# Moving the operand sums and two gate blocks of a Strassen stage into the attention heads before it

## The chip, the cores and the metric

One core of one Trainium2 chip. Times are device microseconds of that core. The kernel was timed in several runs, and one execution of it was taken by the hardware profiler; that one has a span, from its first instruction to its last, and a time of its own.

## The reference, cut to what matters

A block of an encoder on 1024 tokens of 1024 features, in float32. From a normed and modulated `h` one matrix product makes ten groups of 1024 columns, eight blocks of 128 each:

```
proj = h @ w_in[l]
(a_bg, a_cg, a_x, a_z, q, k, v, z_b, a_raw, b_raw, gate_a_raw, gate_b_raw) = split(proj)
ya = a_cg * dwconv_centred(a_bg * a_x, conv_a_w[l]);  ya = (ya * silu(a_z)) @ w_pa[l]
...   # q, k, v: convolution, silu, then 8 heads of a gated delta rule, in both directions: o
yb = (norm(o) * silu(z)) @ w_pb[l]
merged = sigmoid(gate_a_raw) * ya + sigmoid(gate_b_raw) * yb
x = x + gate * (merged @ w_o[l]);  return rmsnorm(x, final_norm_w)
```

## The kernel before, in words

Every large product is made in float32 accuracy from rounded parts: an operand is split into a high and a low part, and a product is three matmuls (high x high, high x low, low x high). The activations `h` lie in SBUF as `hhi`, `hlo` (8 tiles each). A plain block of 128 output columns takes 2 halves x 8 k x 3 = 48 matmuls of 128x512.

**The heads.** q, k, v and z of the eight heads, and the eight blocks of gate a (ga), are projected in plain blocks while the heads' recurrences run. Generators describe the work: `prep_k`, `prep_q`, `merge`, `chain`, `head_out` for each head (chain is the recurrence: 8 steps that go to and fro between TensorE, VectorE and ScalarE; merge completes a triangular inverse that GpSimd forms as many small operations on a tile E), and `fill()` (L1088), one stream of plain blocks. The class `Scheduler` (L59) runs them in Python against a model of costs and writes out a fixed order for each engine. TensorE takes the first stream that is ready, and `fill` stands behind all those of the heads; other engines take, of what is ready, the lowest priority number first. A stream can ask for ("need", name) and goes on when another stream has marked that name.

`fill` keeps a list of main jobs (k, q, v of the next heads, z of the last), each with needs, and a list of gates. `choose()` (L1105) picks the next job while the current one stands ahead; the weights of the job chosen are then loaded by `loader`:

```
share = (total - START - RESERVE) * (mains - len(jobs)) / mains + START
if gates and jobs and total - len(gates) < int(share):
    return gates.pop(0)
if jobs and (len(gates) <= RESERVE or all(n in sched.done for n in jobs[0][3])):
    return jobs.pop(0)
return gates.pop(0) if gates else None
```

The job chosen waits for its needs before its first matmul. z of head h-1 needs ("out", h-2), the mark of `head_out(h-2)` (L1098); z7, the last main job, needs ("out", 6). Its buffer has the tag "tmp" with two buffers, which v and z use in turn.

**The Strassen stage.** The groups bg, ax, cg, az (32 blocks) and two blocks of gate b are projected in pairs of blocks. `Pair` (L1201) makes a pair as seven products of 12 matmuls, 84 in place of 96. Weights are loaded raw (four DMAs a pair), summed (S1 to S4) on VectorE, and each operand is split: `prep` copies the high part on ScalarE, `rest` subtracts for the low part on VectorE, five products ahead (AHEAD). The activations need sums too, T1 to T4, in four rounds m: `sums(m)` (L1169) adds high and low parts of two k-tiles, subtracts four times, and splits the four results. These sums are formed behind the heads, one round beside each of the four plain blocks gb0 to gb3 (`gate_block`, L1367; weights by `wtile`); the loop is at L1374. Then 17 pairs follow, the last of gb4 and gb5, then plain gb6 and gb7, and the output stages.

The heads and this stage are two sections, each with an order of its own on VectorE, ScalarE, GpSimd and SP; rows of the two can interleave. SBUF of the heads (pools `gq`, `gp`) is given to the pools `bw`, `hxp`, `bt` of the stage behind them, tile by tile as readers end.

Of the kernel before, what the change touches and what calls it, by code (L numbers as in the profile page):

```python
# [8 lines left out]
F32 = mybir.dt.float32  # L9
# [315 lines left out]
def block(ctx: ExitStack, tc: tile.TileContext, x, c, wada, wadag, badaT, nwT, win, wab, cva, cvq,  # L325
# [118 lines left out]
    maskF = gc_.tile([P, P], F32, name="maskF")  # L444
    maskB = gc_.tile([P, P], F32, name="maskB")
# [11 lines left out]
    beta = gc_.tile([P, 16, NC], F32, name="beta")  # L457
    exps = gc_.tile([P, 3, 16, NC], F32, name="exps")
    negeg = gc_.tile([P, 16, NC], F32, name="negeg")
    neggc = gc_.tile([P, 16, NC], F32, name="neggc")  # L460
    eg, esuf, gl = exps[:, 0], exps[:, 1], exps[:, 2]

    gq = gctx.enter_context(tc.tile_pool(name="gq", bufs=1))
# [272 lines left out]

    gp = gctx.enter_context(tc.tile_pool(name="gp", bufs=1, reuse_waits="tile"))
# [7 lines left out]
    def big(tag, name, bufs=1):  # L745
        return tile_of(gp, [P, T], tag, name, bufs)
# [341 lines left out]
    def fill():  # L1088
        jobs = []
        for h in range(1, H + 1):  # L1090
            todo = {}
            if 1 < h < H:
                todo["q"] = (Q0 + h, f"q{h}", conv(h, "q", 0), [("chain_e", h - 2)])
            if h + 1 < H:
                todo["k"] = (K0 + h + 1, f"k{h + 1}", conv(h + 1, "k", 8), [("chain_e", h - 2)] if h > 1 else [])
            if h < H:
                todo["v"] = (V0 + h, f"v{h}", conv(h, "v", 16), [("pq", h - 1)])
            todo["z"] = (Z0 + h - 1, f"z{h - 1}", silu_z(h - 1), [("out", h - 2)] if h > 1 else [])  # L1098
            jobs += [todo[c] for c in JOBS if c in todo]
# [69 lines left out]
    def sums(m):  # L1169
        t = []  # L1170
        for k in (2 * m, 2 * m + 1):
            t.append(hxp.tile([P, T], F32, tag="hx", name=f"hx{k}"))
            (V if k % 2 else G).tensor_tensor(t[-1], hhi[k].bitcast(F32), hlo[k].bitcast(F32), ALU.add)
        b11, b12, b21, b22 = (x[:, ch(half, 512)] for x in t for half in range(2))
        V.tensor_tensor(b11, b12, b11, ALU.subtract)
        V.tensor_tensor(b12, b22, b12, ALU.subtract)
        V.tensor_tensor(b22, b22, b11, ALU.subtract)
        V.tensor_tensor(b21, b21, b22, ALU.subtract)
        for n, x in zip(SUMS, (b11, b22, b12, b21)):
            hi, lo = hop[n][m]  # L1180
            S.activation(hi, x, AF.Copy)
            (G if n == "T3" else V).tensor_tensor(lo, x, hi.bitcast(F32), ALU.subtract)
# [18 lines left out]
    class Pair:  # L1201
# [4 lines left out]
        def __init__(self, name, j0, consume, place=None):  # L1206
            self.name, self.consume, self.place = f"{name}{j0}", consume, place
            self.srcs = [win[DST[name] + j0 + b] for b in range(2)]
            self.raw, self.ops, self.banks, self.u = {}, {}, {}, {}
            self.order = {"first": ("A11", "S4", "S2", "A12", "S1", "S3", "A22"),  # L1210
                          "last": ("S2", "S1", "S3", "A22", "A11", "A12", "S4")}.get(place, tuple(RHS))

        def operand(self, n):
            if n not in self.raw:
                if n in ADDS:
                    x, y, op = ADDS[n]
                    x, y = self.operand(x), self.operand(y)
                    t = bw.tile([P, 512], F32, tag="sum", name=f"{n}_{self.name}", bufs=4)
                    V.tensor_tensor(t, x, y, op)
                    self.raw[n] = t  # L1220
                else:
                    for b, a in ((1, 0), (1, 1), (0, 0), (0, 1)):
                        t = bw.tile([P, 512], F32, tag="raw", name=f"wr_{self.name}{b}{a}", bufs=8)
                        Q.dma_start(t, self.srcs[b][:, ch(a, 512)])
                        self.raw[b, a] = t
            return self.raw[n]

# [10 lines left out]
        def product(self, n):  # L1238
            own = (self.place, n) in (("first", "S4"), ("last", "A12"), ("last", "S4"))
# [5 lines left out]
            hi, lo, _ = self.ops.pop(n)  # L1245
# [14 lines left out]
        def after(self, n, ps):  # L1260
# [26 lines left out]
            elif n == "A12":  # L1287
                self.consume(0, 0, ps, None)
# [75 lines left out]
    pairs += [stored("gb", j, sgb_d, AF.Sigmoid, "last" if j + 2 == LAST else None) for j in range(PLAIN[1], LAST, 2)]  # L1364
# [9 lines left out]
    plain = range(*PLAIN)  # L1374
    ws = [wtile(win[G_B + plain[0]], f"gb{plain[0]}")]
    for i, j in enumerate(plain):
        sums(i)
        if j + 1 in plain:
            ws.append(wtile(win[G_B + j + 1], f"gb{j + 1}"))
        else:  # L1380
            for s, (p, n) in enumerate(steps[:4]):
                p.prep(n)
                if s:
                    steps[s - 1][0].rest(steps[s - 1][1])
# [228 lines left out]
```

## Time and profile before

| | us |
|---|---|
| median of 3 runs | 1423.4 (1422.5 to 1424.5) |
| the profiled execution's own time | 1424.3 |
| its span | 1422.5 |
| TensorE busy (PE) | 1371.3, 96% |
| VectorE (DVE) | 852.1, 60% |
| ScalarE (ACT) | 606.6, 43% |
| GpSimd (POOL) | 499.6, 35% |

Time outside the span is 1.8 us in that execution. PE rows are matmuls, PEld their weight loads; a float32 matmul of 128 columns in the heads stands as two rows. Matmuls overlap, so their durations add up to more than the time from one start to the next. The granted clock has two levels, 1.00 (2.4 GHz) and 0.5 (1.2 GHz); a stretch shows a mean. L319 is the line of the helper that records all operations of the heads on engines other than TensorE, L213 that of their matmuls: there one goes by the tiles' names. A name before "<-" is written, those behind it are read; "wl" and "wh" are low and high parts of weights, "wr" raw weights.

### The profile page before, as it was taken

Reading aid. Unit: us, or ns where it says so; the run is one execution under the profiler, and the core shown is the slowest. Engines: PE = TensorE matmul, PEld = TensorE weight load, DVE = VectorE, ACT = ScalarE, POOL = GpSimd, SP = SyncE. Lnnn points to the kernel's source line nnn. Section 1 sums busy time; section 2 is a strip of 40 time slices with the busy share of each in tenths; the row PEclk is TensorE's granted clock in tenths of the full one; section 3 lists DMA queues with packets and bytes.
Section 4 is the critical chain, followed back from the end, with each engine's and each line's share of the span. In section 5 each row is a group of like instructions: output and inputs, shape, how many; then the busy total and the mean of one; then the engine's idle time right before and its main releaser. Section 6 shows DMA issues by size and latency. Waiting matters only on the chain.

```text
span 1422.5 us, 22420 instructions
## 1 busy us (share of the span) xinstructions
PE 1371.3 (96%) x8510; PEld 1145.9 (81%) x8510; DVE 852.1 (60%) x1496; ACT 606.6 (43%) x1490; POOL 499.6 (35%) x728
## 2 busy tenths in 40 slices
PE   6899999999999999998699999999999999999998
PEld 5678888887888887988587788788888788888886
DVE  6868174757686766766326676776767544422335
ACT  5447575565646473745343323232322431222211
POOL 2014837575738384747116100000000123455301
PEclk9999999999999999999899999999999999999999
DMA  9224341514150515132112312103030566665402
GB/s 354 97 70 144 117 95 56 149 39 141 33 146 31 127 54 135 45 75 60 46 45 90 133 45 84 65 24 110 15 119 30 213 231 237 222 200 170 178 16 104
DMA packets 123726, 154.41 MB, mean 109 GB/s; under 512 B 74593, under 2 KB 74977, under 8 KB 123618
## 3 DMA queue, kind: packets, MB, share of 16 engines
q1 hardware_dynamic: 123330, 152.19, 33.6%
q8 instruction: 67, 1.10, 0.3%
q10 hardware_dynamic: 288, 0.79, 0.1%
q14 instruction: 41, 0.34, 0.1%
HBM read 123.45 MB, written 29.50 MB: 108 GB/s over the span
## 4 chain that ended last, share of the span: by engine, by line
PE 46%; POOL 4%; DVE 2%; DMA 2%; issue 1%; ACT 1%; SPq 0%; POOLq 0%; ACTq 0%; DVEq 0%
PE ps_cg_S L1249 4%; PE ps_ax_S L1249 4%; PE ps_az_S L1249 3%; PE ps_bg_S L1249 3%; PE pp_pb L1150 2%; PE pp_pb L1152 2%; PE pp_pa L1152 2%; PE pp_pa L1150 2%; PE pp_pa L1151 2%; PE pp_pb L1151 2%; PE fo L1518 2%; PE fo L1517 2%; PE fo L1519 2%; PE ps_ax_A L1249 2%; PE ps_cg_A L1249 2%; PE pp_ga L213 1%
## 5 line engine op out<-in xcount | busy, mean ns | idle before, releaser
L1142 POOL TENSOR_TENSOR wl_gb<-wr_gb,wh_gb 128x512 fp32r<-128x512 f32 x12 | 19.5, 1646 | 347.8 <-ACT wh_gb L1141 347.8
L319 POOL TENSOR_TENSOR et<-E 128x30 f32<-128x30 f32 (+7 forms) x240 | 112.9, 471 | 28.7 <-DMA E<-s 12.2
L319 POOL TENSOR_TENSOR E<-E,et 128x30 f32<-128x30 f32 (+7 forms) x240 | 114.6, 478 | 17.2
L319 DVE SCALAR_TENSOR_TENSOR S<-S,exps,cb 128x128 f32<-128x128 f32 x96 | 29.7, 343 | 62.0 <-PE cb L213 61.3
L319 ACT ACTIVATE vw<-cb,cols 128x128 f32<-128x128 f32 x112 | 36.0, 364 | 59.1 <-PE cb L213 59.0
L213 PE MATMUL pp_z<-hlo,wh_z 128*128 128x512 f32 x128 | 52.7, 412 | 0.0
L213 PE MATMUL pp_z<-hhi,wl_z 128*128 128x512 f32 x128 | 52.6, 411 | 0.0
L213 PE MATMUL pp_z<-hhi,wh_z 128*128 128x512 f32 x128 | 52.5, 410 | 0.0
L1142 POOL TENSOR_TENSOR wl_pa<-wr_pa,wh_pa 128x512 fp32r<-128x512 f32 x16 | 27.2, 1720 | 71.7 <-ACT wh_pa L1141 37.9
L213 PE MATMUL pp_ga<-hhi,wh_ga 128*128 128x512 f32 x128 | 51.8, 405 | 0.0
L213 PE MATMUL pp_ga<-hhi,wl_ga 128*128 128x512 f32 x128 | 51.8, 405 | 0.0
L213 PE MATMUL pp_ga<-hlo,wh_ga 128*128 128x512 f32 x128 | 51.6, 403 | 0.0
L319 DVE SCALAR_TENSOR_TENSOR r<-cb,negeg,vp 128x128 f32<-128x128 f32 x112 | 35.0, 345 | 26.9 <-PE cb L213 26.2
L1150 PE MATMUL pp_pb<-bhi,wh_pb 128*128 128x512 f32 x128 | 50.4, 394 | 0.0
L1152 PE MATMUL pp_pb<-bhi,wl_pb 128*128 128x512 f32 x128 | 50.2, 392 | 0.0
L1151 PE MATMUL pp_pa<-ylo,wh_pa 128*128 128x512 f32 x128 | 49.8, 389 | 0.0
L1152 PE MATMUL pp_pa<-yhi,wl_pa 128*128 128x512 f32 x128 | 49.8, 389 | 0.0
L1150 PE MATMUL pp_pa<-yhi,wh_pa 128*128 128x512 f32 x128 | 49.8, 389 | 0.0
L1151 PE MATMUL pp_pb<-blo,wh_pb 128*128 128x512 f32 x128 | 49.7, 388 | 0.0
L319 ACT ACTIVATE vn<-cb,cols 128x128 f32<-128x128 f32 x128 | 41.2, 372 | 15.8 <-PE cb L213 15.8
L319 ACT ACT_TABLE_LOAD x36 | 46.2, 1283 | 1.4 <-PEq L1608 0.8
L319 POOL TENSOR_TENSOR wl_ga<-wr_ga,wh_ga 128x512 fp32r<-128x512 f32 x16 | 22.5, 1411 | 68.4 <-ACT wh_ga L319 68.2
(801 smaller groups left out, 4458.9 us busy)
## 6 DMA issues: line engine op xcount, KB each, us to landing
wada<-in_wada SPq DMA_DIRECT2D x16, 512.0 KB, 8.5
D<-gr_d SPq DMA_DIRECT2D x16, 512.0 KB, 6.3
xt<-in_x SPq DMA_DIRECT2D x8, 512.0 KB, 8.5
wr_k<-in_win SPq DMA_DIRECT2D x16, 256.0 KB, 2.6
wr_q<-in_win SPq DMA_DIRECT2D x16, 256.0 KB, 2.6
wr_v<-in_win SPq DMA_DIRECT2D x16, 256.0 KB, 3.5
wr_ga<-in_win SPq DMA_DIRECT2D x16, 256.0 KB, 3.0
qg<-er_d SPq DMA_DIRECT2D x8, 512.0 KB, 6.0
```

The lines of the kernel that those rows point to most:

```text
L213: getattr(self.pe, what)(out, *ins, **kw)
L319: self._sched.record(self._name, lambda: real(*args, **kw), outs, ins, cost, extra, table, op == "memset", port)
L1142: G.tensor_tensor(lo[:, ch(q, 512)], raw, hi[:, ch(q, 512)].bitcast(F32), ALU.subtract)
L1150: PE.matmul(ps, wh, mhi[k][:, sl], start=i == 0, stop=False)
L1151: PE.matmul(ps, wh, mlo[k][:, sl], start=False, stop=False)
L1152: PE.matmul(ps, wl, mhi[k][:, sl], start=False, stop=i == KT - 1)
L1249: PE.matmul(ps, w[:, ch(m)], r, start=first and m == i == 0, stop=m == 3 and i == 2, skip_group_check=True)
L1517: PE.matmul(ps, mhi[k][:, ch(t)], wh, start=k == 0, stop=False)
L1518: PE.matmul(ps, mlo[k][:, ch(t)], wh, start=False, stop=False)
L1519: PE.matmul(ps, mhi[k][:, ch(t)], wl, start=False, stop=k == KT - 1)
```

## The change

RESERVE becomes 4, and gates get two blocks of gate b (EARLY = 2), so ten gates go through `fill` and four are held back to the end of the main jobs. z7 needs ("pq", 7), the mark behind the last vtp matmul of head 7, in place of ("out", 6). Behind the last gate, the weights of bg0 are loaded by the heads' loader. A new stream `early_sums` with priority 4 (the others have 0 to 2) forms rounds 0 and 1 of the sums once ("chain_e", 6) is marked and round 2 once ("chain_e", 7) is; their results go to buffers of heads that are done (the tags ktok, D0, D1, N0, N1, three buffers each, now in a pool `tp` of their own that stays). Round 3 is formed behind the heads. All additions and subtractions of the sums are on VectorE. The four plain blocks between heads and pairs are gone: 18 pairs follow, the last two of gb2 to gb5. The first pair uses bg0's split weights for A11 and A12, and its order is A11, A12, S4, S2, S1, S3, A22. Masks and gate columns move from the pool `gc_` to `gq`.

```diff
-RESERVE = 2
+RESERVE = 4
+ENDING = 0
-PLAIN = (0, 4)
+EARLY = 2
+WHEN = (("chain_e", 6), ("chain_e", 6), ("chain_e", 7))
...
+    def sums(m, raws, V):
+
+        r11, r12, r22, r21 = raw = [t[:, ch(i, 512)] for t in raws for i in range(2)]
+        for r, (odd, half) in zip(raw, ((0, 0), (0, 1), (1, 1), (1, 0))):
+            x, y = (t[2 * m + odd][:, ch(half, 512)].bitcast(F32) for t in (hhi, hlo))
+            V.tensor_tensor(r, x, y, ALU.add)
+        V.tensor_tensor(r11, r12, r11, ALU.subtract)
+        V.tensor_tensor(r12, r22, r12, ALU.subtract)
+        V.tensor_tensor(r22, r22, r11, ALU.subtract)
+        V.tensor_tensor(r21, r21, r22, ALU.subtract)
+
+    def sum_parts(m, tiles, raws, V, S):
+        parts = [(t[:, 0:512], t[:, 512:T]) for t in tiles]
+        raw = [t[:, ch(i, 512)] for t in raws for i in range(2)]
+        for n, (hi, lo), r in zip(SUMS, parts, raw):
+            S.activation(hi, r, AF.Copy)
+            V.tensor_tensor(lo, r, hi.bitcast(F32), ALU.subtract)
+            hop[n][m] = hi, lo
+
+    def early_sums():
+        yield "need", WHEN[0]
+        raws = []
+        for i in range(2):
+            raws.append((yield big("ktok", f"raws{i}", 3)))
+        for m in range(3):
+            yield "need", WHEN[m]
+            tiles = []
+            for tag in ("D0", "D1", "N0", "N1"):
+                tiles.append((yield big(tag, f"sums{m}_{tag}", 3, F32R)))
+            sums(m, raws, V)
+            sum_parts(m, tiles, raws, V, S)
...
-            todo["z"] = (Z0 + h - 1, f"z{h - 1}", silu_z(h - 1), [("out", h - 2)] if h > 1 else [])
+            todo["z"] = (Z0 + h - 1, f"z{h - 1}", silu_z(h - 1), [] if h == 1 else [("out", h - 2)] if h < H else [("pq", h - 1)])
...
-        gates += [(G_B + j, f"gb{j}", activated("gb", j, sgb_d, AF.Sigmoid), []) for j in range(PLAIN[0])]
+        gates += [(G_B + j, f"gb{j}", activated("gb", j, sgb_d, AF.Sigmoid), []) for j in range(EARLY)]
...
-            yield want(*((win[after[0]], after[1]) if after else (None, None)))
+            yield want(*((win[after[0]], after[1]) if after else (win[A_BG], "bg0")))
+            if not after:
+                yield want(None, None)
...
-              + [g for h in range(H) for g in ((prep_k(h), 1), prep_q(h))] + [fill(), loader(2)])
+              + [g for h in range(H) for g in ((prep_k(h), 1), prep_q(h))] + [fill(), loader(2), (early_sums(), 4)])
...
-    hxp = hctx2.enter_context(tc.tile_pool(name="hxp", bufs=2, reuse_waits="tile"))
...
+    hxp = hctx2.enter_context(tc.tile_pool(name="hxp", bufs=1, reuse_waits="tile"))
+    raws = [hxp.tile([P, T], F32, name=f"raws3_{i}") for i in range(2)]
...
-            self.order = {"first": ("A11", "S4", "S2", "A12", "S1", "S3", "A22"),
+            self.order = {"first": ("A11", "A12", "S4", "S2", "S1", "S3", "A22"),
...
-    plain = range(*PLAIN)
-    ws = [wtile(win[G_B + plain[0]], f"gb{plain[0]}")]
-    for i, j in enumerate(plain):
-        sums(i)
...
-        gate_block(j, ws[i])
-    for i in range(4, AHEAD):
+    pairs[0].ops.update((n, [t[:, ch(i, 512)] for t in weights["bg0"]]) for i, n in enumerate(("A11", "A12")))
+    pairs[0].load()
+    sums(3, raws, V)
+    pairs[0].prep("S4")
+    pairs[0].rest("S4")
+    sum_parts(3, [tp.tile([P, T], F32R, tag="ktok", name=f"sums3_{i}", bufs=3) for i in range(3)]
+              + [bw.tile([P, T], F32R, name="sums3_3")], raws, V, S)
+    for i in range(3, AHEAD):
...
```

## Rows read from the trace of the kernel before

**Rows 1.** The page of the profile: busy time of the engines over the span, and of the 40 slices those of TensorE (PE, busy tenths) and of its granted clock (PEclk, tenths of full speed).

```profile
PE 1371.3 (96%) x8510; PEld 1145.9 (81%) x8510; DVE 852.1 (60%) x1496; ACT 606.6 (43%) x1490; POOL 499.6 (35%) x728
...
PE   6899999999999999998699999999999999999998
...
PEclk9999999999999999999899999999999999999999
```

**Rows 2.** The table by stage: start and end in us, length, then busy time (and instructions) of PE, PEld, DVE, ACT and POOL, mean granted clock, DMA share and GB/s. The stretches are the end of the heads before head 7's z, the rest of the heads, the plain gate blocks, the first pair, and the 15 pairs behind it up to the pair of gates.

```profile
662.80:694.30 31.50, 16.15 (x256) 14.16 (x254) 11.57 (x38) 11.92 (x42) 17.63 (x43) 0.78 0.11 18
694.30:747.50 53.20, 53.20 (x367) 46.39 (x366) 15.23 (x48) 20.82 (x62) 6.67 (x5) 1.00 0.15 50
747.50:793.70 46.20, 44.78 (x194) 35.81 (x193) 30.93 (x34) 16.72 (x30) 28.40 (x14) 1.00 0.29 103
793.70:817.76 24.06, 21.36 (x85) 16.77 (x84) 14.55 (x23) 7.70 (x14) 0.00 (x0) 0.93 0.38 131
817.76:1108.91 291.15, 290.75 (x1261) 236.41 (x1260) 206.55 (x307) 84.12 (x143) 0.00 (x0) 1.00 0.18 60
```

**Rows 3.** The waits of TensorE from 660 to 700 us, the two longest: who waited for whom, us in all, times, longest.

```profile
PE psy L213 <- DVE T L319: 8.8, 1, 8.8
PE cb L213 <- ACT vn L319: 3.7, 4, 1.3
```

**Rows 4.** The timeline of TensorE around its gaps: start, us, what, and the idle time before it with what ended it.

```profile
662.32 0.48 PE L213 MATMUL pp_z<-hhi,wl_z 128*128 128x512 f32 x1
...
677.44 0.75 PE L213 MATMUL o<-vn,D 128*128 128x128 f32 x4 [0.26 <-ACT vn L319]
686.94 0.31 PE L213 MATMUL psy<-T,N 32*32 32x32 f32 x2 [8.76 <-DVE T L319]
...
694.29 0.47 PE L213 MATMUL pp_z<-hhi,wh_z 128*128 128x512 f32 x1
```

**Rows 5.** The table by stage for the stretch from the end of the long gap to head 7's z, columns as in rows 2.

```profile
687.00:694.30 7.30, 4.69 (x169) 3.84 (x169) 5.49 (x17) 1.24 (x3) 0.00 (x0) 0.52 0.16 26
```

**Rows 6.** The instructions on the tile vtp of head 7 (v transposed), from 640 to 662 us: count, duration min/median/max in ns, first and last start in us.

```profile
L213 PE MATMUL vtp<-ident,vT x8: 272/272/273, 655.1 to 657.0; 128*128 128x128 f32 x8
```

**Rows 7.** TensorE's instructions by line from 694.3 to 747.5 us, the two groups of 64 rows: count, busy us, mean ns, idle before.

```profile
L213 PE MATMUL psz<-T,N 64*64 64x64 f32 x32 | 1.1, 221 | 0.0
L213 PE MATMUL psv<-N,y 64*64 64x64 f32 x32 | 1.1, 221 | 0.0
```

**Rows 8.** The same from 662.8 to 694.25 us, the two groups of psy.

```profile
L213 PE MATMUL psy<-T,N 32*32 32x32 f32 x32 | 1.6, 238 | 10.4 <-DVE T L319 8.8 <-ACT T L319 1.6
...
L213 PE MATMUL psy<-y,N 32*32 32x32 f32 x32 | 1.4, 238 | 1.0 <-DVE y L319 0.8
```

**Rows 9.** Busy time of the instructions on the banks cb alone, over chain 6 and over chain 7 (columns PE, PEld, DVE, ACT, PEclk, DMA share, GB/s): the length of the stretch is that of the chain.

```profile
645.60:677.30 31.70, 14.90 (x88) 13.12 (x88) 8.54 (x28) 8.41 (x30) 1.00 0.09 29
701.50:735.60 34.10, 13.34 (x88) 13.01 (x87) 8.42 (x28) 8.19 (x29) 1.00 0.05 16
```

**Rows 10.** Instructions by line and shape from 747.5 to 800 us, three groups of VectorE in the sums: count, busy us, mean ns, idle before.

```profile
L1173 DVE TENSOR_TENSOR hx<-hhi,hlo 128x1024 f32<-128x1024 f32 x4 | 7.8, 1947 | 0.1
...
L1175 DVE TENSOR_TENSOR hx<-hx 128x512 f32<-128x512 f32 x4 | 2.8, 692 | 14.8 <-POOL hx L1173 14.8
...
L1182 DVE TENSOR_TENSOR T1l<-hx,T1h 128x512 fp32r<-128x512 f32 x4 | 2.7, 684 | 0.0
```

**Rows 11.** The table by stage from 676 to 701 us, columns as in rows 2.

```profile
676.00:701.00 25.00, 13.37 (x264) 10.73 (x264) 10.58 (x29) 7.42 (x27) 6.08 (x18) 0.73 0.25 62
```

**Rows 12.** The timeline behind chain 7, several engines: start, us, what, idle before it and what ended it (SPq rows are DMA issues).

```profile
741.54 0.17 DVE L319 SCALAR_TENSOR_TENSOR oss<-oss,qss 128x8 f32<-128x8 f32 x1 [6.94 <-ACT sqj L319]
...
745.68 1.03 PE L213 MATMUL otp<-ident,vp 128*128 128x128 f32 x8
...
746.32 1.41 DVE L319 SCALAR_TENSOR_TENSOR sz<-otp,gnw_t,sz 128x512 f32<-128x512 f32 x2 [0.56 <-PE otp L213]
...
747.75 0.33 SPq L319 DMA_DIRECT2D yb_d<-sz  x1
...
750.51 2.41 POOL L1173 TENSOR_TENSOR hx<-hhi,hlo 128x1024 f32<-128x1024 f32 x1 [6.44 <-DMA yb_d<-sz]
```

**Rows 13.** The timeline of SP's queue: the issue of a plain gate block's weights and the first store of ga6's gate row behind it.

```profile
714.95 1.56 SPq L1140 DMA_DIRECT2D wr_gb<-in_win  x2
735.51 0.33 SPq L319 DMA_DIRECT2D sga_d<-xpad  x1
```

**Rows 14.** The timeline of TensorE at the first pair's first product.

```profile
796.14 0.57 PE L1249 MATMUL ps_bg_A<-hhi,wloA_bg 128*128 128x512 f32 x1 [1.82 <-DVE wloA_bg L1236]
```

**Rows 15.** The timeline of the first round of sums: one subtraction on GpSimd, one on VectorE.

```profile
756.42 1.78 POOL L1182 TENSOR_TENSOR T3l<-hx,T3h 128x512 fp32r<-128x512 f32 x1 [3.49 <-DVE T1l L1182]
...
756.95 1.79 DVE L1182 TENSOR_TENSOR T4l<-hx,T4h 128x512 fp32r<-128x512 f32 x1
```

**Rows 16.** The timeline of GpSimd, the first and the last of the 14 operations, on et and E in turn, that head 7's inversion still has from 676.2 us on.

```profile
676.27 0.35 POOL L319 TENSOR_TENSOR et<-E 128x84 f32<-128x84 f32 x1
...
681.12 0.23 POOL L319 TENSOR_TENSOR E<-E,et 128x15 f32<-128x15 f32 x1
```

**Rows 17.** The chain of work that ended last, from 747 to 800 us: the first VectorE operation behind the additions in the first and in the last of the four rounds of sums (start, us).

```profile
752.96 0.70 DVE hx L1175
...
787.64 0.70 DVE hx L1175
```

More of the change, by code (lines that the diff above doesn't have):

```diff
@@ L443, in block @@
     gctx.enter_context(tc.manual_schedule(engines=others))
-    maskF = gc_.tile([P, P], F32, name="maskF")
-    maskB = gc_.tile([P, P], F32, name="maskB")
+    gq = gctx.enter_context(tc.tile_pool(name="gq", bufs=1))
+    maskF = gq.tile([P, P], F32, name="maskF")
+    maskB = gq.tile([P, P], F32, name="maskB")
     G.memset(maskF, 0.0)
@@ L456, in block @@
         G.memset(xp[:, T + 2 : T + 4], 0.0)
[L457 to L460, printed above, removed]
+    beta = gq.tile([P, 16, NC], F32, name="beta")
+    exps = gq.tile([P, 3, 16, NC], F32, name="exps")
+    negeg = gq.tile([P, 16, NC], F32, name="negeg")
+    neggc = gq.tile([P, 16, NC], F32, name="neggc")
     eg, esuf, gl = exps[:, 0], exps[:, 1], exps[:, 2]
-    gq = gctx.enter_context(tc.tile_pool(name="gq", bufs=1))
     tiles = {}
@@ L743, in block, with big @@
     et = gp.tile([P, 128], F32, name="et")
-    def big(tag, name, bufs=1):
-        return tile_of(gp, [P, T], tag, name, bufs)
+    def big(tag, name, bufs=1, dtype=F32):
+        return tile_of(gp if bufs < 3 else tp, [P, T], tag, name, bufs, dtype)
+    SUMS = ("T1", "T3", "T2", "T4")
+    hop = {n: [None] * 4 for n in SUMS}
+    def sums(m, raws, V):
[26 more added lines that the diff above has]
+            sum_parts(m, tiles, raws, V, S)
     npad = [2]
@@ L1108, in choose @@
                 return gates.pop(0)
-            if jobs and (len(gates) <= RESERVE or all(n in sched.done for n in jobs[0][3])):
+            if jobs and (len(gates) <= (RESERVE if len(jobs) > ENDING else 0) or all(n in sched.done for n in jobs[0][3])):
                 return jobs.pop(0)
@@ L1188, in block @@
     DST = {"ga": G_A, "gb": G_B, "z": Z0, "bg": A_BG, "ax": A_X, "cg": A_CG, "az": A_Z}
-    place, spare = [-7 * (17 + (LAST - PLAIN[1] - 2) // 2) % 6], []
+    place, spare = [2], []
     def slots(name):
@@ L1221, in operand, with load @@
                 else:
[L1222 to L1225, printed above, removed]
+                    self.load()
             return self.raw[n]
+        def load(self):
+            for b, a in ((1, 0), (1, 1), (0, 0), (0, 1)):
+                self.raw[b, a] = bw.tile([P, 512], F32, tag="raw", name=f"wr_{self.name}{b}{a}", bufs=8)
+                Q.dma_start(self.raw[b, a], self.srcs[b][:, ch(a, 512)])
         def prep(self, n):
@@ L1238, in product @@
         def product(self, n):
-            own = (self.place, n) in (("first", "S4"), ("last", "A12"), ("last", "S4"))
+            own = self.place and n in ("A12", "S4")
             pl = po if own else BANK[n]
@@ L1287, in after @@
             elif n == "A12":
-                self.consume(0, 0, ps, None)
+                self.consume(0, 0, ps, u["e1"] if first else None)
             elif n == "A22":
@@ L1363, in block @@
     pairs = [mixed(n, j, None if i else "first") for i, (n, j) in enumerate(pairs)]
-    pairs += [stored("gb", j, sgb_d, AF.Sigmoid, "last" if j + 2 == LAST else None) for j in range(PLAIN[1], LAST, 2)]
+    pairs += [stored("gb", j, sgb_d, AF.Sigmoid, "last" if j + 2 == LAST else None) for j in range(EARLY, LAST, 2)]
     steps = [(p, n) for p in pairs for n in p.order]
@@ L1372, in gate_block @@
         Q.dma_start(sgb_d[j], xp[:, 2 : T + 2])
-    plain = range(*PLAIN)
-    ws = [wtile(win[G_B + plain[0]], f"gb{plain[0]}")]
-    for i, j in enumerate(plain):
-        sums(i)
[L1378 to L1384, printed above, removed]
-        gate_block(j, ws[i])
-    for i in range(4, AHEAD):
+    pairs[0].ops.update((n, [t[:, ch(i, 512)] for t in weights["bg0"]]) for i, n in enumerate(("A11", "A12")))
[6 more added lines that the diff above has]
+    for i in range(3, AHEAD):
         steps[i][0].prep(steps[i][1])
-        steps[i - 1][0].rest(steps[i - 1][1])
+        if i > 3:
+            steps[i - 1][0].rest(steps[i - 1][1])
     hctx2.close()
```

24 lines of the change are left out of this document (3 added, 21 removed).

## The prediction, made before the result was known

> **What bounds the kernel now.** I read the busy shares and the 40 slices first. TensorE is busy 96% of the span, so time can come only from its gaps, its slow clock, or fewer matmuls; the slices put gap and slow clock together in the 19th and 20th slice [rows 1]. The table by stage shows what these stretches are [rows 2]: 662.8 to 694.3 us is the end of the heads before z of head 7 starts (16.15 us busy of 31.50, granted clock 0.78 on average), 694.3 to 747.5 is head 7 with fill (no gap), 747.5 to 793.7 the four plain gate blocks, 793.7 to 817.76 the first Strassen pair, and from there 15 pairs run at 291.15 / 15 = 19.4 us each, 0.231 us a matmul.
>
> The waits of TensorE in that first stretch are 8.8 us for a transposition (DVE T) and 3.7 us for ScalarE's vn of chain 6 [rows 3]. Neither names the cause. The cause is that no fill stands there: the last fill matmul (pp_z of head 6) starts at 662.32, then only chain 6 steps, then nothing from 677.44 to 686.94, and the next fill, head 7's z, comes only behind otp of head 6 [rows 4]. In the code, fill() takes z7 as the last main job while two gates are still held back, and z7 needs ("out", 6), that is head_out of head 6. The two gates wait behind it. The gap also lowers the granted clock to 0.52 in the stretch that follows it, near the 1.2 GHz level (0.5) [rows 5].
>
> **The change, part by part.**
>
> z7 released. Its need becomes ("pq", 7), met when head 7's last vtp matmul is issued; that one starts at 657.0 [rows 6], so z7 follows z6 at once. Reserve goes from 2 to 4 and gates from 8 to 10; since 10 - 4 - 4 = 8 - 4 - 2, the share of gates spread over the earlier jobs is unchanged, and I expect the order up to z6 to be the old one. After z6 the fill is then z7, ga6, ga7, gb0, gb1: 5 blocks of 48 matmuls instead of 3.
>
> Where the heads end on TensorE, if fill never runs out. Head 7's stretch, without a gap, holds 367 matmuls [rows 2]: 144 of fill (3 blocks), 64 psz and psv in 2.2 us [rows 7], 159 of 128 columns. 53.2 - 144 x 0.231 = 19.9 us are head work, so those 159 take (19.9 - 2.2) / 159 = 0.111 us each. The stretch before it holds 256: one of fill, 160 of 32 columns, 95 of 128 columns, 10.5 us. Of the small ones psy's 64 were busy for 3.0 us at the low clock [rows 8]; for all 160 at full clock I take 2.4. So 662.8 + 12.9 + 19.9 + 240 x 0.231 (55.4) = 751.0 us. Bounds: 748 (the head's work packs better) and 756 (5 us of stops).
>
> Is head 7 done by then? Head 7's merge starts at 686.94 on VectorE's transposition, which follows the inversion and not the fill [rows 4]; chain 7 took 34.1 us with fill beside it [rows 9], and otp of head 7 stood at 745.68. Chain 6 becomes slower (it ran 31.7 us, partly alone), about 6 us by the other pace, and ends at about 683; merge 7 doesn't wait for that, and chain 7, which does, began at 701.5 [rows 9]. So fill (to 751.0) covers the old finish with 4 to 5 us to spare.
>
> Sums in the heads. A round is 12 VectorE operations of 128x512 (in the old form 1 of 128x1024 and 7 of 0.7 us, with 2 more on GpSimd [rows 10]), so 12 x 0.69 = 8.2 us, and 4 ScalarE copies as before. Rounds 0 and 1 may start when chain 6 is recorded, round 2 with chain 7. VectorE is busy 10.58 of 25 us in 676 to 701 and 8.42 of 34.1 in chain 7's own work [rows 9, 11]: 14.4 and 25.7 us are idle, so 16.4 fit, at the lowest priority. What hides them is that idle time; if it were gone they would cost 8.2 us each behind the heads. An operation that has begun is not interrupted, so a step of merge or chain can wait 0.7 us; with some ten such hits otp moves to 747 to 751. I take 749. Round 2 (8.2 us) falls in 736 to 748, where VectorE waits 6.94 us for sqj, then for otp [rows 12].
>
> Queues. SP carries the same weight loads, two blocks of them earlier, plus bg0's; the gates' stores keep their size. Rows of the second section stand ahead of rows of the heads in SP's queue already (wr_gb at 714.95 before sga_d at 735.51) [rows 13], so the first pair's four raw loads need not queue behind gb1's store; if they do, they land some 5 us later, within the bound below.
>
> Plain blocks gone, one pair more. Before, pairs begin at 793.7; after, at 751.0. The 18th pair costs 84 x 0.231 = 19.4 us, against 96 matmuls for its two plain blocks.
>
> The first pair's own loss. Before it took 24.06, 4.7 over a pair: 1.82 us is a gap for VectorE's wloA, the rest smaller waits and a granted clock of 0.93 in the mean [rows 2, 14]. After, A11 and A12 need neither sums nor loads (bg0 is prepared in the heads), 24 x 0.231 = 5.5 us, to 756.5. S4 needs its weights, and VectorE's order is sums(3), then S1, S2, S4. sums(3) writes to a buffer whose place, by the sizes in the code, falls at the tail of the buffer that z7 holds; so it waits for yb_d of head 7 to be read. Before, exactly that wait is seen: hx of GpSimd for 6.44 us on yb_d, issued 747.75, over at 750.5 [rows 12]. With otp at 749: sz 750.4, yb_d 753.1, 8 operations to 758.6, three sums to 760.7, ScalarE's copy to 761.3: S4 is some 5 us late. A low clock followed such gaps before: 24.06 x (1 - 0.93) = 1.7 us in the first pair, 7.3 x (1 - 0.52) = 3.5 us behind the 8.76 us gap of head 7 [rows 2, 5]. I take 7 us. Bounds: 0 (buffer free, sums done by 748) and 12 (loads late too). T2 of round 3 is third of four halves, 4 x 0.69 = 2.8 us after S4's, while S4's 12 matmuls run 2.8 us: nothing more.
>
> Sum: (751.0 + 7) - (793.7 + 4.7) + 19.4 = -21.0 us. The end (gb4,5 pair, gb6, gb7, output) keeps its work. The profiled execution took 1424.3 us around a span of 1422.5; the median of three runs is 1423.4, 0.9 less. 1423.4 - 21.0 = 1402.4.
>
> **A rule beside a row.** VectorE's T4l took 1.79 us where T1l takes 0.68 [rows 10], with GpSimd's T3l in progress from 756.42 to 758.20 [rows 15]: the one waited until the other ended. The sums are all of this kind. The Trainium skill, SBUF — State Buffer, section "Who interferes with whom", says that a VectorE instruction with two SBUF inputs and a GpSimd instruction that reads SBUF exclude each other for the whole instruction; by that rule the trace agrees, and rival A is what it would do here.
>
> **The rivals.**
>
> A. Sums stop GpSimd's inversion of head 7. Its last 14 operations run from 676.27 to 681.35 at 0.22 to 0.35 us, and merge 7 hangs on them [rows 16]. If round 0 starts at 676 there, 13 of them wait 0.69: 9 us. Then otp stands at 755, yb_d over at 759, S4's weights at 767: 10.6 us of gap and 3.5 of clock, 14.1 in place of 7: 1423.4 - 13.9 = 1409.5. Against: chain 6, slowed by z7, is recorded some 6 us later than before. Chance 0.13.
>
> B. The change doesn't do what it says: z7 still waits (for a buffer of its tag). Then all of 662.8 to 747.5 stays, gb0 and gb1 add 96 x 0.231 = 22.2 us, pairs begin at 769.7 with the old 4.7: 769.7 - 793.7 + 19.4 = -4.6, so 1418.8. Chance 0.06.
>
> C. Slower: the lowest priority leaves all four rounds behind the heads, on VectorE alone. In the old program a round came every 11.56 us [rows 17]; four from 747.7 end at 793.9, S4's weights at 796.7 against 756.5, 40.2 us and 3.5 of clock: 751.0 + 43.7 - 798.4 + 19.4 = +15.7, 1439. It is slower than before from 7.6 us a round on. For: it is last in priority and in order. Against: VectorE's idle time above, and tiles of heads 5 and 6 that are free by then. Chance 0.05.
>
> **How the numbers follow.** The forecast has 0.72; 0.04 is for losses that add up to no change. Range: low with the first pair at 0 and the heads at 748 gives 1392.4; I stop at 1394, since both together are rare. High: 12 in the first pair and 5 us of stops in the heads, 1412, which holds rival A; rivals B and C and the 0.04 stay out. A measurement here can tell 0.2% (2.8 us) from no change. Faster: 0.72 + 0.13 + 0.06 = 0.91; slower 0.05; same 0.04.
>
> **What would show it.** In the profile after: no gap of TensorE over 1.5 us between 660 and 745 and a granted clock of 1.00 there; z7 directly behind z6; matmuls of gb0 and gb1 within the heads (line of the helper, L213 before), and no plain gate block until gb6; the first ps_bg at 748 to 756; raws and sums of rounds 0 and 1 on VectorE before 735; one gap of some 5 us ahead of S4 of bg, and 18 pairs of 19.4 us. It is wrong if the first ps_bg stands after 760, if merge 7 starts after 692, or if S2 waits for sums.

## The result, and the profile after the change

The change made the kernel faster: 1408.13 us (median of 4 runs, 1407.14 to 1408.63) against 1423.05 us for the kernel before in the same session, a ratio of 0.9893 [0.9875, 0.991]. The profiled execution took 1408.43 us around a span of 1406.7; that of the kernel before took 15.9 us more. The forecast was 1402.4 in a range of 1394 to 1412: the sign and the range held, the gain came out 14.9 us instead of 21.0.

The table by stage of the kernel after (columns as in [rows 2]). The stretches are: from the end of z of head 6 to the end of z of head 7; from there to the end of the heads; the first pair; 16 further pairs; the pair of gates.

```profile
662.80:683.06 20.26, 20.26 (x131) 18.23 (x131) 6.21 (x18) 6.61 (x21) 15.42 (x40) 1.00 0.06 11
683.06:753.86 70.80, 68.29 (x586) 58.04 (x584) 44.91 (x103) 37.42 (x105) 14.03 (x10) 1.00 0.22 72
753.86:782.90 29.04, 21.53 (x86) 16.86 (x86) 22.80 (x36) 8.24 (x15) 0.00 (x0) 0.88 0.43 145
782.90:1093.92 311.02, 310.90 (x1349) 253.09 (x1348) 221.34 (x330) 93.19 (x156) 0.00 (x0) 1.00 0.19 65
1093.92:1113.24 19.32, 18.63 (x81) 14.96 (x81) 5.66 (x9) 6.46 (x12) 5.09 (x4) 1.00 0.56 194
```

Against [rows 2], stretch by stage: z of head 7 now stands directly behind z of head 6, TensorE is busy without a break at a granted clock of 1.00 where it was busy 16.15 of 31.50 us at 0.78, and the first pair starts at 753.86 instead of 793.7 (39.8 us earlier). The first pair takes 29.04 us instead of 24.06 (5.0 lost). The 17 pairs behind it take 311.02 + 19.32 = 330.34, 19.43 each, 19.0 more than the 16 of before. What follows takes 293.5 against 293.4. Sum, with the second decimal kept: -39.84 + 4.98 + 19.0 + 0.06 = -15.8 us, the difference of the two spans.

The waits of TensorE from 660 to 700 us, where [rows 3] had 8.8 and 3.7 us, and then its timeline at every gap from there to the end of the first pair:

```profile
PE psu L215 <- DVE Vb L321: 1.0, 1, 1.0
```

```profile
697.76 0.23 PE L215 MATMUL psu<-N,Vb 32*32 32x32 f32 x4 [1.04 <-DVE Vb L321]
...
751.89 0.30 PE L215 MATMUL otp<-ident,vp 128*128 128x128 f32 x1 [1.06 <-DVE vp L321]
752.60 0.72 PE L215 MATMUL otp<-ident,vp 128*128 128x128 f32 x3 [0.41 <-DVE vp L321]
...
766.25 0.80 PE L1272 MATMUL ps_bg_S<-hhi,whiS_bg 128*128 128x512 f32 x1 [6.64 <-ACT whiS_bg L1254]
...
780.05 0.70 PE L1272 MATMUL ps_bg_S<-sums_N,whiA_bg 128*128 128x512 f32 x2 [0.88 <-DVE u_bg L1281]
```

The 8.76 us gap of [rows 4] is gone. What remains of the heads is 2.5 us in three gaps; the new large gap is the one ahead of S4, 6.64 us. Behind it a stretch at the lower clock level is left, as a table of 6.8 us shows (columns as before; 3.35 us of it busy, granted clock 0.50):

```profile
762.80:769.60 6.80, 3.35 (x8) 2.64 (x9) 5.98 (x10) 3.75 (x7) 0.00 (x0) 0.50 0.26 92
```

Why S4 is late is read from VectorE's timeline behind head 7, and SP's queue beside it:

```profile
753.63 1.40 DVE L321 SCALAR_TENSOR_TENSOR sz<-otp,gnw_t,sz 128x512 f32<-128x512 f32 x2
758.14 2.50 DVE L760 TENSOR_TENSOR raws<-hhi,hlo 128x512 f32<-128x512 f32 x4 [3.11 <-DMA yb_d<-sz]
...
762.73 0.69 DVE L764 TENSOR_TENSOR raws<-raws 128x512 f32<-128x512 f32 x1
763.34 0.68 DVE L1240 TENSOR_TENSOR S_bg<-wr_bg,wr_bg 128x512 f32<-128x512 f32 x1
...
766.23 0.69 DVE L1259 TENSOR_TENSOR wloS_bg<-S_bg,whiS_bg 128x512 fp32r<-128x512 f32 x1 [0.76 <-ACT whiS_bg L1254]
```

```profile
755.06 0.32 SPq L321 DMA_DIRECT2D yb_d<-sz  x1
755.44 2.24 SPq L1249 DMA_DIRECT2D wr_bg<-in_win  x4
```

This is the chain of the forecast, link by link: sz of head 7, its store yb_d, round 3 (which writes where the stored tile lay), three sums, ScalarE's copy. It is the wait of [rows 12] in a new place, on VectorE instead of GpSimd.

And why the heads end late: VectorE's timeline around merge 7, whose first operation is the transposition T<-N.

```profile
686.56 0.69 DVE L321 TENSOR_TENSOR raws<-raws 128x512 f32<-128x512 f32 x1
688.79 0.17 DVE L321 SCALAR_TENSOR_TENSOR oss<-oss,qss 128x8 f32<-128x8 f32 x1 [1.53 <-ACT sqj L321]
...
689.43 1.30 DVE L321 TENSOR_TENSOR oss<-oss,qss 128x8 f32<-128x8 f32 x1
690.65 0.68 DVE L321 TENSOR_TENSOR sums_D<-raws,sums_D 128x512 fp32r<-128x512 f32 x1
691.25 0.89 DVE L321 STREAM_TRANSPOSE T<-N 32x256 f32<-32x256 f32 x2
```

The busy time on the banks cb alone, over chain 6 and chain 7, answers to [rows 9] (same columns):

```profile
645.92:683.01 37.09, 14.94 (x88) 14.64 (x88) 8.89 (x28) 8.31 (x29) 1.00 0.11 27
707.93:742.82 34.89, 13.34 (x88) 13.01 (x87) 8.37 (x28) 8.12 (x29) 1.00 0.18 65
```

With z of head 7 beside it chain 6 takes 37.1 us instead of 31.7. The oss operations of head 6 follow its end, and in VectorE's order they stand ahead of T<-N; so merge 7 begins late, and its psy matmuls come at 694.38 instead of 686.94 (the last of them at 694.9 instead of 691.3). Chain 7 starts 6.4 us later than before and otp of head 7 comes 6.2 us later, at 751.89.

### The profile page after: what moved, and what is told of

The parts are those of the page before. It is cut to its first block, busy times and chain, and to the rows that moved or that the text cites. A ratio compares the mean times of both kernels' runs of the same rounds, so it can differ in the third digit from the quotient of the medians.

```text
span 1406.7 us, 22408 instructions
## 1 busy us (share of the span) xinstructions
PE 1365.2 (97%) x8498; PEld 1142.4 (81%) x8498; DVE 867.2 (62%) x1527; ACT 607.8 (43%) x1493; POOL 475.8 (34%) x718
## 4 chain that ended last, share of the span: by engine, by line
PE 88%; DVE 5%; ACT 2%; DMA 2%; issue 1%; POOL 1%; SPq 0%; POOLq 0%; DVEq 0%; ACTq 0%
PE pp_z L215 6%; PE pp_v L215 6%; PE pp_ga L215 6%; PE pp_q L215 5%; PE cb L215 5%; PE ps_cg_S L1272 4%; PE ps_ax_S L1272 4%; PE o L215 4%; PE ps_az_S L1272 4%; PE ps_bg_S L1272 4%; PE pp_k L215 3%; PE pp_pb L1191 2%; PE pp_pb L1193 2%; PE pp_pa L1192 2%; PE pp_pa L1193 2%; PE pp_pa L1191 2%
## 5 line engine op out<-in xcount | busy, mean ns | idle before, releaser
L1183 POOL TENSOR_TENSOR wl_gb<-wr_gb,wh_gb 128x512 fp32r<-128x512 f32 x4 | 5.1, 1292 | 354.9 <-ACT wh_gb L1182 354.9
L321 POOL TENSOR_TENSOR E<-E,et 128x30 f32<-128x30 f32 (+7 forms) x240 | 119.2, 497 | 17.2
L321 POOL TENSOR_TENSOR et<-E 128x30 f32<-128x30 f32 (+7 forms) x240 | 108.8, 454 | 26.0 <-DMA E<-s 9.5
L215 PE MATMUL pp_v<-hlo,wh_v 128*128 128x512 f32 x112 | 45.7, 408 | 0.0
```

The source lines that it names most:

```text
L215: getattr(self.pe, what)(out, *ins, **kw)
L321: self._sched.record(self._name, lambda: real(*args, **kw), outs, ins, cost, extra, table, op == "memset", port)
L1183: G.tensor_tensor(lo[:, ch(q, 512)], raw, hi[:, ch(q, 512)].bitcast(F32), ALU.subtract)
```

## The experiments

Ten kernels were run. Times within two runs are shifted against each other as a whole, by up to 7 us (z of head 6 starts at 637.52 in experiment 2, at 638.77 in the changed kernel and at 644.58 in experiment 5); below, lengths are compared, or that start is used to remove the shift. Rows are shown as they stand in their run. The kernel before took 1424.75 to 1425.36 us (medians) in these sessions. Verdicts are by the ratio to it; the change itself stands at 0.9893.

**1. Does the gain come from z of head 7?** Its old need is put back, all else stays.

```
-   ... [("out", h - 2)] if h < H else [("pq", h - 1)])
+   ... [("out", h - 2)])
```

> The changed kernel with z of head 7 needing (out, 6) again, all else kept. My theory (the release of z7 is what fills the old gap): TensorE stands idle again for some 15 us between 663 and 695 and runs at the low clock behind it, z7 starts behind otp of head 6, the heads end some 770 us on, but the first pair finds its sums done and loses 1 to 2 us in place of 9.6: 1415 to 1419. Rival (the sums being hidden carry the gain, z7 little): at most 1411.

Measured: 1421.63 us, 0.9984 [0.9971, 0.9997]. Nearly the whole gain is gone: without the release of z7 the other parts of the change bring next to nothing. (Experiments 5 and 6 take out other parts and lose the gain too, so the release is needed, but is not shown to be enough; it was not tried alone.) The time lies 2.6 us above the theory's upper end: the gap is longer than before, and GpSimd's timeline shows one reason, since a round of sums now meets head 7's inversion.

```profile
676.31 0.34 POOL L321 TENSOR_TENSOR E<-E,et 128x78 f32<-128x78 f32 x1
676.73 0.66 POOL L321 TENSOR_TENSOR et<-E 128x65 f32<-128x65 f32 x1
...
681.68 0.66 POOL L321 TENSOR_TENSOR E<-E,et 128x30 f32<-128x30 f32 x1
682.42 0.22 POOL L321 TENSOR_TENSOR et<-E 128x15 f32<-128x15 f32 x1
```

TensorE's gap in the same run, against 8.76 us in [rows 4]:

```profile
688.48 0.31 PE L215 MATMUL psy<-T,N 32*32 32x32 f32 x2 [10.50 <-DVE T L321]
```

While VectorE does the round's eight operations on raws (676.35 to 682.23), eight operations of GpSimd take 0.58 to 0.66 us each instead of 0.23 to 0.34, 2.8 us more in all. That is rival A's mechanism, at some 0.35 us an operation. The sums delay more than that: they stand among VectorE's scalings of head 6's vp, and z of head 7 starts at 698.42, 4.1 us later than in [rows 4], so the stretch at the lower clock level is longer as well (a granted clock of 0.50 from 688.5 to 701.8).

```profile
698.42 0.78 PE L215 MATMUL pp_z<-hhi,wh_z 128*128 128x512 f32 x1
```

**2. Four early gate blocks instead of two**, and 17 pairs.

```
-RESERVE = 4        +RESERVE = 6
-EARLY = 2          +EARLY = 4
-place, spare = [2], []
+place, spare = [3], []
```

> Two more blocks of gate b in the heads (EARLY 4, RESERVE 6), so 17 pairs behind them. My theory (the first pair loses 9.6 us because S4 waits for round 3 of the sums, which waits for the store of yb of head 7): the two blocks, 22.2 us of TensorE, stand over that wait, the first pair takes 19.4 to 21 us, and the whole is 2.8 us of matmuls more and some 8 to 10 us of waiting less: 1400 to 1402. Rival (VectorE's amount of work at the start of the pairs is the bound, not the wait): the gap moves along, 1409 to 1411.

Measured: 1407.63, 0.9879 [0.9864, 0.9894]; neither. The first pair is 27.6 us long, with 4.32 us of gap ahead of S4. SP's queue says why:

```profile
762.87 10.98 SPq L321 DMA_DIRECT2D sgb_d<-xpad  x2
773.89 2.25 SPq L1249 DMA_DIRECT2D wr_bg<-in_win  x4
```

The last gate's store waits in SP's queue for the last gate block, and the first pair's raw loads stand behind it. VectorE then sat 13.51 us idle until they landed, though round 3 was long done. The gap did not shrink, it got another cause.

**3. Round 3's buffers moved off the stored tile**, by 1 KB of padding ahead of them.

```
+    hxp.tile([P, 256], F32, name="pad")
     raws = [hxp.tile([P, T], F32, name=f"raws3_{i}") for i in range(2)]
```

> The buffers of round 3 moved by 1 KB, off the tail of the buffer that z7 holds, nothing else. My theory: round 3 on VectorE no longer waits 3.1 us for the store of yb of head 7 and starts at about 755 in place of 758.1; the gap ahead of S4 shrinks from 6.6 to 3.5 us: 1404 to 1405.5. Rival (VectorE's work or the raw weights' landing bounds S4): less than 1 us of change, 1407.5 to 1408.5.

Measured: 1406.68, 0.9877 [0.9858, 0.9895]. Round 3 starts directly behind sz (759.23, no wait), and the gap ahead of S4 falls from 6.64 to 2.68 us; the first pair takes 26.83 instead of 29.04. The time lies between the theory and the rival. The gain is 1.5 us by the medians, 2.3 by the ratios and 2.2 by the first pair, but the intervals of the two ratios overlap: the wait's place is shown by the trace, its price only roughly.

```profile
759.23 2.50 DVE L760 TENSOR_TENSOR raws<-hhi,hlo 128x512 f32<-128x512 f32 x4
```

```profile
768.14 0.50 PE L1273 MATMUL ps_bg_S<-hhi,whiS_bg 128*128 128x512 f32 x1 [2.68 <-ACT whiS_bg L1255]
```

The next limits show at once: VectorE waits 0.84 us for a raw load, and the work behind sz is itself longer than TensorE's cover.

**4. Rounds 0 and 1 held until merge 7 is recorded**, so that no sum stands ahead of it.

```
-WHEN = (("chain_e", 6), ("chain_e", 6), ("chain_e", 7))
+WHEN = (("merged", 7), ("merged", 7), ("chain_e", 7))
```

> Rounds 0 and 1 of the sums may start only when merge 7 is recorded, so none of them stands ahead of merge 7 on VectorE. My theory (merge 7 is late, 694.4 in place of 686.9, mainly because chain 6, slowed by z7, has its last small steps ahead of the transpositions in VectorE's order): the transpositions come at 689 to 690 in place of 691.2, merge 7 gains 1.5 us at most, total 1406 to 1409. Rival (round 0 alone makes merge 7 late): transpositions at 686 to 687, merge and chain 7 some 5 us earlier, the gap ahead of otp of head 7 gone, 1404 to 1405.5.

Measured: 1409.16, 0.989 [0.9874, 0.9906]: no gain. VectorE's timeline, with no sums in it:

```profile
683.81 0.61 DVE L321 SCALAR_TENSOR_TENSOR r<-cb,negeg,vp 128x128 f32<-128x128 f32 x2 [0.74 <-PE cb L215]
691.15 0.17 DVE L321 SCALAR_TENSOR_TENSOR oss<-oss,qss 128x8 f32<-128x8 f32 x1 [6.73 <-ACT sqj L321]
...
693.01 0.89 DVE L321 STREAM_TRANSPOSE T<-N 32x256 f32<-32x256 f32 x2
```

VectorE sits idle for 6.73 us, waiting for ScalarE's squares of head 6, and merge 7 starts at 693.01; this run's z of head 6 started 2.34 us later, so that is 690.7 against 691.25 (689 to 690 was expected). The sums cost merge 7 0.6 us; the rest is chain 6, which ends later, and its oss operations in front of T<-N. The rival fell.

**5. All rounds of sums behind the heads**: what hiding them is worth, and rival C on the chip.

```
+WHEN = (("out", 7), ("out", 7), ("out", 7))
```

> The changed kernel with rounds 0 to 2 of the sums held until head_out of head 7 is recorded, so that all four rounds stand behind the heads on VectorE. My theory (the hiding is worth its 8.2 us a round): three rounds more ahead of S4's weights, S4 some 22 to 25 us later than in the changed kernel, 1428 to 1434. Rival (the sums are not on the path that sets the end, or they slowed the heads as much as they cost behind them): 1408 to 1415.

Measured: 1423.86, 0.999 [0.998, 1.0]. The whole change without hidden sums is worth nothing, though the time lies between the two ranges. The gap ahead of S4 is 17.95 us and the first pair 45.7 long, 16.6 more than in the change. Against that, the pairs begin at 751.6 (shift removed) instead of 753.86: so the hiding is worth 16.6 - 2.3 = 14.3 us, and by the ratios 13.8. The mechanism is there; its price is less than the 20 to 26 us expected. TensorE's rows at otp of head 7 and at S4, and VectorE's at S4's sums:

```profile
755.60 1.03 PE L215 MATMUL otp<-ident,vp 128*128 128x128 f32 x8
...
781.00 0.79 PE L1272 MATMUL ps_bg_S<-hhi,whiS_bg 128*128 128x512 f32 x1 [17.95 <-ACT whiS_bg L1254]
```

```profile
779.54 0.68 DVE L1240 TENSOR_TENSOR S_bg<-wr_bg,S_bg 128x512 f32<-128x512 f32 x1
780.14 0.68 DVE L321 TENSOR_TENSOR raws<-hhi,hlo 128x512 f32<-128x512 f32 x1
```

The rows of the two sections interleave on VectorE. Round 3 and the sums of S4's weights (L1240) run between the other rounds, and nine of the twelve operations of round 2 come only behind S4's last sum. So S4 does not stand behind three more whole rounds.

**6. No early gate blocks**, and 19 pairs.

```
-RESERVE = 4        +RESERVE = 2
-EARLY = 2          +EARLY = 0
-place, spare = [2], []
+place, spare = [1], []
```

> z7 released and sums in the heads as in the changed kernel, but no block of gate b in the heads (EARLY 0, RESERVE 2): the fill behind z6 is z7, ga6, ga7, and 19 pairs follow. My theory (the heads end with head 7's chain, which fill only accompanies; the two blocks are free there): the heads end 751 to 753 us on with 15 us of idle TensorE ahead, and the 19th pair costs 19.4: 1422 to 1428. Rival (the heads end when the fill ends, the two blocks were not free): 1404 to 1408.

Measured: 1421.47, 0.9981 [0.997, 0.9991]: 0.5 us under the theory's range, but its picture holds only in part. Fill ends with ga7 at 717.4, chain 7 then runs almost alone (26.7 us instead of 34.9), and TensorE waits 7.93 us for otp of head 7.

```profile
746.04 1.94 PE L215 MATMUL otp<-ident,vp 128*128 128x128 f32 x8 [7.93 <-DVE vp L321]
```

Less the shift, the heads end at 745.3, not at the 751 to 753 expected, against 753.9 in the change: two gate blocks, 96 x 0.231 = 22.2 us of matmuls, moved the heads' end by 8.6. They were not free, but they cost less than the 19th pair that takes their place.

**7. Experiment 2 with the first pair's raw loads on ScalarE's queue.**

```
-                Q.dma_start(self.raw[b, a], ...)
+                (nc.scalar if self.place == "first" else Q).dma_start(self.raw[b, a], ...)
```

> The run with four blocks of gate b in the heads, and the first pair's four raw loads issued on ScalarE's queue in place of SP's, where they stood behind the store of the last gate. My theory (in that run S4 waited only for those loads): no gap ahead of S4, the first pair takes 19.4 to 21 us, 1399 to 1401.5. Rival (VectorE's work ahead of S4, or ScalarE's own order, holds S4 as well): 1405 to 1408.

Measured: 1409.16, 0.9886 [0.9871, 0.9901]: no gain, and 1.2 us above the rival's range. ScalarE issued them at 774.08, behind its copy of the last gate's bank, which starts at 774.07 and has waited 4.90 us for the matmuls.

```profile
774.07 0.60 ACT L321 ACTIVATE xpad<-pp_gb 128x512 f32<-128x512 f32 x1 [4.90 <-PE pp_gb L215]
774.08 1.92 ACTq L1249 DMA_DIRECT2D wr_bg<-in_win  x4
```

An in-order queue was exchanged for another one that waits for the same gate block. VectorE waits 15.0 us for wr_bg, in three waits.

**8. Two gates, loads on ScalarE's queue, S4 prepared ahead of round 3, padding as in 3.**

```
     pairs[0].load()
-    sums(3, raws, V)
     pairs[0].prep("S4")
     pairs[0].rest("S4")
+    sums(3, raws, V)
```

> The changed kernel with three edits at the first pair: its raw loads on ScalarE's queue, S4's sums ahead of round 3 on VectorE, and round 3's buffers moved off z7's. My theory (first pair's 9.6 us are all waiting in queues and for one buffer): S4's weights ready by 759, round 3 by 764, no gap over 1.5 us, first pair 19.4 to 21.5: 1398 to 1400.5. Rival (VectorE's amount of work bounds it): the gap moves from S4 to S2, 1404 to 1407.

Measured: 1409.43, 0.9892 [0.9875, 0.9908]: the rival's picture, 2.4 us above its range; the ratio is that of the change. TensorE's gaps in the first pair:

```profile
760.42 0.50 PE L1273 MATMUL ps_bg_S<-hhi,whiS_bg 128*128 128x512 f32 x1 [0.89 <-ACT whiS_bg L1255]
767.51 1.22 PE L1273 MATMUL ps_bg_S<-sums_N,whiS_bg 128*128 128x512 f32 x2 [3.79 <-ACT whiS_bg L1255]
769.34 0.80 PE L1273 MATMUL ps_bg_S<-sums_N,wloS_bg 128*128 128x512 f32 x1 [0.60 <-DVE wloS_bg L1260]
```

The gap moved from S4 to S2, which now waits for round 3. With two gates VectorE takes 13.7 us from the end of sz of head 7 (754.95) to S2's low part (768.60), 3.4 of them waits, and TensorE has 8.3 us of products (A11, A12, S4) to cover it: this other order only moved the loss.

**9. Four gates, the last gate's store issued behind the raw loads**, and the padding of 3. Four gates put some 18 us of gate blocks between otp of head 7 and the first pair; this frees the loads from SP's queue.

```
     def activated(name, j, dst_d, func):
+        npad[0] += name == "gb" and j == EARLY - 1 and npad[0] % 3 == 2
...
+        if name == "gb" and j == EARLY - 1:
+            held.append((dst_d[j], xp[:, 2 : T + 2]))
+        else:
+            Q.dma_start(dst_d[j], xp[:, 2 : T + 2])
...
     pairs[0].load()
+    Q.dma_start(*held[0])
     sums(3, raws, V)
```

> Four early gate blocks, as in e2, but the store of the last of them is issued by SP behind the first pair's four raw loads instead of ahead of them (it leaves from another of the three padded buffers, so that it holds up nothing), and round 3's buffers lie 1 KB further, as in e3. Theory: what was left of the first pair's loss with four gates was only the queue: the loads, issued at 773.9 in e2 behind a store that waited 11 us, now go out by some 763 and land by 768, about when round 3's sums end there (766.2); VectorE forms S1, S2 and S4 at once, and ScalarE rounds S4 as soon as the last gate block's copy (774.1) is done, some 5 us ahead of the time TensorE comes to S4 (about 781). No gap ahead of S4, first pair 19.4 to 21 long in place of 27.6: 1399.5 to 1401.5. Rival (VectorE's and ScalarE's serial work behind head 7 bounds the first pair whatever the loads do, as it did with two gates in e8): the gap moves on from S4 to S2, first pair 24 to 28, 1404 to 1408.

Measured: 1399.8 (1399.25 to 1404.99), 0.9837 [0.9821, 0.9853], as the theory has it. SP's queue, two rows of VectorE and the table of the first pair:

```profile
758.43 1.88 SPq L1256 DMA_DIRECT2D wr_bg<-in_win  x4
...
776.20 0.33 SPq L1406 DMA_DIRECT2D sgb_d<-xpad  x1
```

```profile
764.42 0.69 DVE L1247 TENSOR_TENSOR S_bg<-wr_bg,wr_bg 128x512 f32<-128x512 f32 x1 [2.51 <-DMA wr_bg<-in_win]
...
774.16 0.69 DVE L1266 TENSOR_TENSOR wloS_bg<-S_bg,whiS_bg 128x512 fp32r<-128x512 f32 x1 [6.61 <-ACT whiS_bg L1261]
```

```profile
773.48:793.93 20.45, 19.57 (x85) 15.68 (x84) 14.82 (x23) 8.30 (x15) 0.00 (x0) 1.00 0.45 155
```

The loads go out at 758.43 instead of 773.89, S4's sums are done at 767.54 and VectorE then waits 6.61 us for ScalarE's copy of them, TensorE has no gap ahead of S4, the clock stays at 1.00 and the first pair takes 20.45 us. Its interval lies wholly below that of the change: this version beats both kernels.

**10. The same without the padding.**

> e9 without the 1 KB shift: round 3's buffers lie where the change put them, under head 7's gate tile. It tells which of e9's two edits took the first pair's loss away. Theory: the place of the store alone. In e9 VectorE then waited 6.6 us for ScalarE's copy of S4 (which stands behind the last gate block), so 3 us more of waiting for yb_d are covered: no gap ahead of S4, first pair 19.4 to 21 long, 1399 to 1401.5. Rival: both are needed, since round 3's later end pushes the splits behind S4 and the gap returns ahead of S4 or S2, 2 to 4 us of it: 1402 to 1404.

Measured: 1402.09 (1401.03 to 1403.8), 0.9836 [0.9818, 0.9854]. Round 3 again waits 3.09 us for yb_d, TensorE has no gap in the first pair but the 0.9 us late in it that experiment 9 has too, and the pair is 20.44 us long. By the ratios, which take out the session, the two are the same: the place of the store does it alone, and VectorE's 3 us are covered.

## Why the prediction was right, and where it was too hopeful

**z of head 7 released: right.** It stands directly behind z of head 6; no gap over 1.04 us from 660 to 745 and a granted clock of 1.00 there, as the forecast asked. Experiment 1 shows that without it the other parts hardly pay (0.9984).

**Heads end at 751.0: too early by 2.9 us.** The count of TensorE's work was right: less its 2.5 us of gaps the stretch ends at 751.4. The step that failed is the next one: for the end of chain 6, "merge 7 doesn't wait for that". Merge 7 needs head 7's inversion, whose result DMAs carry into N. In the kernel before, T<-N waited 3.10 us for them; the prediction took the start of psy, 686.94, for that of T<-N:

```profile
686.45 0.90 DVE L319 STREAM_TRANSPOSE T<-N 32x256 f32<-32x256 f32 x2 [3.10 <-DMA N<-s]
```

In the kernel after, the inversion was on time (its last operation ended at 680.6, before at 681.35 [rows 16]), and so were these DMAs, which before were issued at 684.66:

```profile
683.93 1.80 SPq L321 DMA_DIRECT2D N<-s  x4
```

But on VectorE's queue merge 7 stands behind the oss operations of head 6, and these behind chain 6, which z of head 7 slows, by 5.4 us, about as forecast. So merge 7 does wait for chain 6: T<-N came at 691.25 and psy at 694.38 (a start of merge 7 after 692 was named as a sign of error).

Experiment 5, which has no sums in the heads, gives the price. Its otp of head 7 comes at 755.60 - 5.81 = 749.79 (shift removed), 4.1 us later than in the kernel before, TensorE has no gap at it, and the pairs begin at 751.6. So of the 6.2 us by which otp came later in the change, some 4.1 are there without any sums, and the forecast had nothing for them; the sums add 2.1, for which it had 3.3. Fill covers the first alone, but not both: that is the 1.5 us of gap at otp. Experiment 4 shows that of the sums' part 0.6 us falls at the start of merge 7. It was not tried to change the order on VectorE.

**Sums hidden: right in the main.** Rounds 0 and 1 ran from 682 to 714, round 2 from about 742 to 752, mostly in VectorE's idle time, each operation 0.68 to 0.69 us. Against experiment 5 they let the heads end 2.3 us later and save 16.6 us in the first pair: hiding them is worth about 14 us.

**First pair's loss: the right mechanism, 9.6 us instead of 7.** Its chain ran through the same links, from otp at 751.89 (forecast 749) to the S4 copy's end at 766.2 (761.3). TensorE's start was 2.9 late as well, so the gap grew by less, from 4.8 to 6.64: from the start of otp to the end of sz the forecast gave 1.4 us, the length of sz alone, where [rows 12] have 2.05 (745.68 to 747.73); it took 3.1, since VectorE still scaled vp between (its last scaling ran until 753.7). Then 0.88 us for u_bg, which was not counted, and an estimated 1.7 of low clock: 3.35 us of the 6.8 at 0.50 were busy, and half of them is lost. That makes 9.2 of the 9.6.

**The remark on SP's queue** was that the raw loads "need not queue" behind the last gate's store. With two gates they did not (issued 755.44, behind yb_d only). With four they did, and cost more than the 5 us named there: 13.51 us of VectorE's idling in experiment 2.

**18th pair: right**, 19.0 against 19.4.

Added up: 2.9 (heads) + 2.6 (first pair) - 0.4 (18th pair) = 5.1, and 0.1 in what follows: the -15.8 measured against the -21.0 forecast.

**The rivals.** A did not happen in the change: the sums began at 682.0, after the inversion's last operation, for the reason given against it. Experiment 1 shows it at work where chain 6 ends earlier, at about 0.35 us an operation, not 0.69. The Trainium skill, SBUF — State Buffer, section "Who interferes with whom", says that a VectorE instruction with two SBUF inputs contends with a GpSimd instruction that reads SBUF, and that the shared ports are an exclusive lock. The trace agrees that the two slow each other down, but not by whole instructions: eight operations of GpSimd lost 0.35 us each, half of a VectorE operation, and the eight VectorE operations beside them took 5.88 us instead of 5.26 in the change. Rival B is experiment 1, in effect, and its 1418.8 was 2 to 3 us too low. Rival C's mechanism is experiment 5: the first pair lost 45.7 - 19.4 = 26.3 us there, not 43.7, because VectorE went through 40 operations without a wait from 755.58 to 780.14, 0.61 us each and so some 7.4 us a round rather than 11.56, and because most of round 2 came behind S4's sums. With these 26.3 and the pairs' start at 751.6, rival C's own sum gives 751.6 + 26.3 - 798.4 + 19.4 = -1.1 us, and the ratio was 0.999: not slower than before, so its sign was wrong.

## What to carry to other kernels

The parts of such a change do not add up one by one: with z7 held, with the sums unhidden or without the two gate blocks, nearly the whole gain was gone each time. Fill that is moved into a gap slows the chain beside it, and whatever stands behind that chain on another engine's fixed order comes late with it: before calling a step independent, read what is ahead of it on its own queue. Then look at the first stage behind a removed section: what had been prepared under its cover (loads, sums, splits) now needs a cover of its own, and one more block of plain work of known length may pay for itself there. And a load that waits on nothing still waits for the store ahead of it in its queue: issue the loads first, and changing to another in-order queue helps only if that one does not wait for the same thing.

## What the runs showed of the hardware that was not expected

- Short gaps already cost clock. After TensorE's gap of 2.68 us in experiment 3 the granted clock was 0.57 in the mean over the eight matmuls behind it; after 4.32 us in experiment 2 it was 0.50 over eight; after the 0.88 us gap in experiment 9 it stayed at 1.00.
- Fill beside a head's chain costs only part of its own length: chain 7 takes 26.7 us almost alone, with fill 34.9. Two more gate blocks of 22.2 us moved the end of the heads by 8.6 us (experiment 6).
- One store that waited for TensorE held four unrelated loads back in SP's queue until 773.89 us (experiment 2), and a ScalarE copy that waited for TensorE did the same in ScalarE's (experiment 7).
